# Gated linear attention beside a projection: four gate pieces of a head, one to each half chunk of weights

## The chip, the cores and the metric

The kernel runs on one core of one Trainium2 chip. The metric is the device time of one execution in microseconds (us); the median of three runs of the kernel before is 1993.54 us.

## The reference

One layer of a diffusion backbone: 256 latent tokens and 256 context tokens, width 2048, all in float32. One input projection feeds two token mixers, windowed attention and a bidirectional gated linear attention (GLA) of four heads; their merged output goes through a convolutional FFN. The change touches the GLA alone:

```python
gf = log_sigmoid((lrf @ w_gate_f + b_gate_f)) / GLA_GATE_NORM     # decay, forward; gb the same, backward
...
def step(S, inp):                       # one chunk of 64 tokens, scanned forward and backward
    qc, kc, vc, gc = inp
    b = cumsum(gc)
    o_inter = (qc * exp(b)) @ S
    A[t, s] = sum_d qc[t,d] * kc[s,d] * exp(b[t,d] - b[s,d])      # s <= t
    o = o_inter + A @ vc
    S = exp(b[last]) * S + (kc * exp(b[last] - b)).T @ vc
```

The context gives the states in which the latent scans start. Of each head the key width is 256 and the value width 512.

## The kernel before

Nearly all the time goes into products of the tokens with weights that are read once. Weights come in chunks of 256 rows x 512 columns. ScalarE (ACT) rounds a chunk to `whi` (L227), VectorE (DVE) takes the rest `wlo` (L228), and TensorE (PE) multiplies first with `whi` (the high products), then with `wlo` (the low products). Three buffers each hold `whi` and `wlo`, so the next `whi` can be written only when PE is through with the high products of an earlier chunk, and the next `wlo` only after its low products.

The GLA of a head, without its value product, is a generator, `gla_A`. It runs beside a projection of eight chunks: beside that of the other keys for head 0, beside that of its own values for heads 1 to 3. The projection calls `aside` twice in each chunk, once ahead of the high products (`tick`) and once between high and low ones (`midway`). These 16 places are called slots here: odd ones lie ahead of high products, even ones between high and low. `aside` adds the pace to a sum, and each time that the sum reaches one it lets `gla_A` run on to its next `yield`. PE's instructions of a step are placed behind the last product issued before the slot; those of ACT and DVE are free. A scheduler then settles each engine's order from its own model of times, and every engine works through its order strictly.

The steps of `gla_A` are these. **Gates**: for two directions d and two halves dt of the key width, a product `pz` on PE, then four activations of 128x512 on ACT (L720, L722, L723, L724), then a sum on DVE (L725, into `segs`) and one on GpSimd (POOL, L726, into `gc`). **Levels** 0 to 7: exponentials of `segs` on ACT (L765, L766, and from level 1 on L772, L773), products with queries and keys on DVE (`q2` L767, `k2` L774), and up to four sums on DVE that carry `segs` to the next level (L776 to L779). **Products**: `products(lv)` multiplies `k2` by `q2` of a level on PE into `pa`, and a masked copy on DVE (L750) takes it; called p0 to p7 here. p0 needs only `q2` of level 0. `q2` and `k2` share four buffers, so a level's exponentials wait for the products of the level two below. **End**: two queries, four scans and `kf` (L807), `kg` (L808) on DVE, an empty step, then the final products of `kf` and `kg` on PE (the `pa<-q,kf` of the trace) that give `atc`.

With pace 0.91 the slots of a head hold:

| slot | before |
|---|---|
| 2 | two gates (d = 0) |
| 3 | two gates (d = 1) |
| 4 | first `pa`, level 0 |
| 5 | level 1 |
| 6 | p0 |
| 7 to 11 | levels 2 to 6, each with the product of the level below (p1 to p5) |
| 12 | nothing |
| 13 | level 7, p6 |
| 14 | p7, queries, scans, `kf`, `kg` |
| 16 | final products |

A background job on DVE (L385, 128x1024, some 1.2 us a piece) computes the modulation vectors; the scheduler fits its pieces in between.

Of the kernel before, what the change touches and what calls it, by code (L numbers as in the profile page):

```python
# [30 lines left out]
def layer_kernel(ctx, tc, A, out):  # L31
# [18 lines left out]
    def M(name, shape, dt=F32):  # L50
        return big.tile(shape, dt, name=name, tag="M")

    def W2(tag, name, shape, dt=F32):
        return f2.tile(shape, dt, name=name, tag=tag, bufs=F2_BUFS[tag])

    def bank(name, shape=(P, 512), side=False):

        return ps.tile(list(shape), F32, name=name, tag="side" if side else "main", bufs=3 if side else 1)

    def split(hi, lo, src):  # L60
        S.activation(hi, src, AF.Copy)
        return V.tensor_tensor(lo, src, hi.bitcast(F32), op=ALU.subtract).ins
# [31 lines left out]
    def mm_b(*a, **k):  # L94
        return pe_seq(after(PE.matmul(*a, **k)))  # L95
# [70 lines left out]
    beside = []  # L166
# [537 lines left out]
    def gla_A(h, kb, qb, res):  # L704
        k_ = kb[:, (h % 2) * 2:(h % 2) * 2 + 2, 0:T]
        kc = kb[:, (h % 2) * 2:(h % 2) * 2 + 2, T:2 * T]
        q_ = qb[:, 2 * h:2 * h + 2, :]
        R = M("segs", [P, 4, 2, T])
        PF, SB, SX, PX = (R[:, i] for i in range(4))
        G.memset(R[:, 2:4], 0.0)  # L710
        gc = []
        for d in range(2):
            g_ = W2("fc", "gc", [P, 2, T])
            for dt in range(2):
                f = 2 * h + dt
                pz = bank("pz", side=True)
                mm_b(pz, wg[:, f * P:(f + 1) * P], lr[:, d, :], start=True, stop=True)
                b = nbg[:, d * 8 + f:d * 8 + f + 1]
                e = W2("fb", "ge", [P, 512])
                S.activation(e, pz, AF.Abs, scale=-1.0, bias=b)  # L720
                mn = W2("fb", "gm", [P, 512])
                S.activation(mn, pz, AF.Relu, scale=-1.0, bias=b)  # L722
                S.activation(e, e, AF.Exp, scale=-1.0)  # L723
                S.activation(e, e, AF.Ln, bias=ones[:, 0:1])  # L724
                V.tensor_tensor((PF if d == 0 else SB)[:, dt, :], mn[:, 0:T], e[:, 0:T], op=ALU.add)  # L725
                G.tensor_tensor(g_[:, dt, :], mn[:, T:2 * T], e[:, T:2 * T], op=ALU.add)  # L726
            gc.append(g_)
            yield

        at = sm.tile([P, 2, P], F32, name="at", tag="at", bufs=1)  # L730
        pa = bank("pa", (P, 2, P), side=True)
        for t in range(2):
            for dt in range(2):
                mm_b(pa[:, t, :], k_[:, dt, t * P:(t + 1) * P], q_[:, dt, t * P:(t + 1) * P],
                          start=(dt == 0), stop=(dt == 1))
        V.tensor_scalar(at, pa, 2.0, None, op0=ALU.mult)

        def halves(x, m):
            v = x.rearrange("p d (n two h) -> p (d n) two h", two=2, h=m)
            return v[:, :, 0, :], v[:, :, 1, :]  # L740

        def products(lv, q2, k2):
            pa = bank("pa", (P, 2, P), side=True)
            for t in range(2):
                tq = t if lv < 7 else 1 - t
                for dt in range(2):
                    mm_b(pa[:, t, :], k2[:, dt, t * P:(t + 1) * P],
                              q2[:, dt, tq * P:(tq + 1) * P], start=(dt == 0), stop=(dt == 1))
            if lv < 7:
                V.copy_predicated(at, lmask[:, lv:lv + 1, :].to_broadcast([P, 2, P]), pa)  # L750
            else:
                split(ats[0][:, 0], ats[0][:, 1], at)
                split(ats[1][:, 0], ats[1][:, 1], pa)

        ats = [W2("fc", "ats", [P, 2, 2, P], F32R) for _ in range(2)]
        for lv in range(8):
            m = 1 << lv
            n = T // m
            pfL, pfR = halves(PF, m)
            sbL, sbR = halves(SB, m)  # L760
            sxL, sxR = halves(SX, m)
            pxL, pxR = halves(PX, m)
            q2 = W2("fa", "q2", [P, 2, T])
            qL, qR = halves(q2, m)
            S.activation(qR, pfR, AF.Exp, scale=-1.0 / 16)  # L765
            S.activation(qL, sbL, AF.Exp, scale=-1.0 / 16)  # L766
            V.tensor_tensor(q2, q2, q_, op=ALU.mult)  # L767
            k2 = k_
            if lv:
                k2 = W2("fa", "k2", [P, 2, T])  # L770
                kL, kR = halves(k2, m)
                S.activation(kL, sxL, AF.Exp, scale=-1.0 / 16)  # L772
                S.activation(kR, pxR, AF.Exp, scale=-1.0 / 16)  # L773
                V.tensor_tensor(k2, k2, k_, op=ALU.mult)  # L774
            if lv < 7:
                V.tensor_tensor(sxL, sxL, pfR[:, :, m - 1:m].to_broadcast([P, n, m]), op=ALU.add)  # L776
                V.tensor_tensor(pxR, pxR, sbL[:, :, 0:1].to_broadcast([P, n, m]), op=ALU.add)
            V.tensor_tensor(pfR, pfR, pfL[:, :, m - 1:m].to_broadcast([P, n, m]), op=ALU.add)
            V.tensor_tensor(sbL, sbL, sbR[:, :, 0:1].to_broadcast([P, n, m]), op=ALU.add)  # L779
            if lv == 1:  # L780
                yield
            if lv:
                products(lv - 1, *prev)
            prev = q2, k2
            yield
        products(7, *prev)


        q2 = W2("fa", "q2", [P, 2, T])
        q3 = W2("fa", "q3", [P, 2, T])  # L790
        for dst, e in ((q2, PF), (q3, SB)):
            S.activation(dst, e, AF.Exp, scale=-1.0 / 16)
            V.tensor_tensor(dst, dst, q_, op=ALU.mult)
        kf = W2("fa", "kf", [P, 2, T])
        kg = W2("fa", "kg", [P, 2, T])
        tot = sm.tile([P, 2], F32, name="tot", tag="tot", bufs=2)
        one = ones[:, 0:1].to_broadcast([P, T])
        for dt in range(2):
            V.tensor_tensor_scan(kf[:, dt, :], one, gc[0][:, dt, :], 0.0, op0=ALU.mult, op1=ALU.add)
            V.memset(kg[:, dt, 0:1], 0.0)  # L800
            V.tensor_tensor_scan(kg[:, dt, 1:T], ones[:, 0:1].to_broadcast([P, T - 1]), gc[1][:, dt, 0:T - 1], 0.0,
                                 op0=ALU.mult, op1=ALU.add)
        V.tensor_scalar(tot, kf[:, :, T - 1], -1.0 / 16, None, op0=ALU.mult)
        for dt in range(2):
            S.activation(kf[:, dt, :], kf[:, dt, :], AF.Exp, scale=1.0 / 16, bias=tot[:, dt:dt + 1])
        S.activation(kg, kg, AF.Exp, scale=-1.0 / 16)
        V.tensor_tensor(kf, kf, kc, op=ALU.mult)  # L807
        V.tensor_tensor(kg, kg, kc, op=ALU.mult)  # L808
        yield
        yield  # L810
        pa = bank("pa", (P, 2, T), side=True)
        for t in range(2):
            for i, (kk, qq) in enumerate(((kf, q2), (kg, q3))):
                for dt in range(2):
                    mm_b(pa[:, t, :], kk[:, dt, t * P:(t + 1) * P], qq[:, dt, :],
                              start=(i == 0 and dt == 0), stop=(i == 1 and dt == 1))
        atc = [W2("fc", "atc", [P, 2, T], F32R) for _ in range(2)]
        split(atc[0], atc[1], pa)
        res.extend((ats, atc))
# [32 lines left out]
    qbt = M("qb", [P, 8, T])  # L852
# [2 lines left out]

    def with_gla(h, kb, block):
        res = []
        beside[:] = [gla_A(h, kb, qbt, res), 0.91, 0.0]
        v = block()
        for _ in beside[0]:  # L860
            pass
        beside.clear()
        return res, v

    def kb_block():
        kb = M("kb1", [P, 4, 512])
        proj_T(w_in, KB + 512, ALL, [h_all(0), h_all(1)], lambda i, b: S.activation(kb[:, i, :], b, AF.Copy))
        return kb

    a, kb1 = with_gla(0, kbt, kb_block)  # L870
    v = M("v0h", [P, 4, 512], F32R), M("v0l", [P, 4, 512], F32R)
    for i in range(4):
        split(v[0][:, i, :], v[1][:, i, :], vb0[:, i, :])
    gla_o(0, a, *v)
    for h in (1, 2, 3):
        a, v = with_gla(h, kb1 if h > 1 else kbt, lambda h=h: v_block(VB + h * 512, f"v{h}", h == 3))
        if h < 3:
            gla_o(h, a, *v)
# [424 lines left out]
```

## Time and profile before

| | |
|---|---|
| median of three runs | 1993.54 us (1993.23 to 1993.6) |
| profiled execution | 1993.73 us, of it a span of 1991.7 us |
| PE busy | 1965.2 us (99%) |
| DVE busy | 1401.9 us (70%) |
| ACT busy | 971.1 us (49%) |
| granted TensorE clock | 0.998 |
| GLA heads 0, 1, 2, 3 in the span | from 224, 287, 351, 415 us, each until 52 to 55 us later |

The start of a head is its first `pz` on PE. A wait of PE in this kernel is time lost, since PE is busy almost everywhere. A wait of DVE or ACT costs nothing by itself; it matters where PE later waits for what was held up. In rows of the timeline the number behind `x` counts the instructions merged into the row, and the bracket gives the idle time ahead of it on its engine, with what ended it.

### The profile page before, as it was taken

Reading aid. Unit: us, or ns where it says so; the run is one execution under the profiler, and the core shown is the slowest. Engines: PE = TensorE matmul, PEld = TensorE weight load, DVE = VectorE, ACT = ScalarE, POOL = GpSimd, SP = SyncE. Lnnn points to the kernel's source line nnn. Section 1 sums busy time; section 2 is a strip of 40 time slices with the busy share of each in tenths; the row PEclk is TensorE's granted clock in tenths of the full one; section 3 lists DMA queues with packets and bytes.
Section 4 is the critical chain, followed back from the end, with each engine's and each line's share of the span. In section 5 each row is a group of like instructions: output and inputs, shape, how many; then the busy total and the mean of one; then the engine's idle time right before and its main releaser. Section 6 shows DMA issues by size and latency. Waiting matters only on the chain.

```text
span 1991.7 us, 27308 instructions
## 1 busy us (share of the span) xinstructions
PE 1965.2 (99%) x10393; PEld 1644.6 (83%) x10393; DVE 1401.9 (70%) x2164; ACT 971.1 (49%) x1417; POOL 48.5 (2%) x69
## 2 busy tenths in 40 slices
PE   6999999999999999999999999999999999999999
PEld 5779897878887788888888888888888888888887
DVE  4666568867858898777776458888887555667754
ACT  4323464653345566444444445755555334555532
POOL 1001000111000000000000000000000000000000
PEclk9999999999999999999999999999999999999999
DMA  9987223235754455888888768688886566666563
GB/s 324 385 293 212 66 75 95 85 99 188 241 174 127 117 180 187 269 291 289 291 289 285 237 220 283 180 264 275 270 269 233 195 195 190 188 186 188 189 215 113
DMA packets 199699, 420.89 MB, mean 211 GB/s; under 512 B 12660, under 2 KB 21156, under 8 KB 198416
## 3 DMA queue, kind: packets, MB, share of 16 engines
q1 hardware_dynamic: 197808, 413.25, 64.3%
q0 software_dynamic: 1696, 5.89, 1.0%
q8 instruction: 81, 1.33, 0.3%
q14 instruction: 50, 0.41, 0.1%
q10 hardware_dynamic: 64, 0.02, 0.0%
HBM read 416.97 MB, written 2.13 MB: 210 GB/s over the span
## 4 chain that ended last, share of the span: by engine, by line
PE 93%; DVE 3%; ACT 2%; issue 1%; DMA 1%; POOL 0%; SPq 0%; POOLq 0%; DVEq 0%; ACTq 0%
PE acc L83 71%; PE accs L83 12%; PE pa L95 2%; PE pm L95 1%; PE poa L95 1%; PE pS L95 1%; PE po L95 1%; PE ptp L98 1%; DVE wlo L228 1%; DMA mraw<-in_w_mod 1%; PE plr L677 0%; PE pto L98 0%; ACT ge L720 0%; ACT whi L227 0%; DVE raw L385 0%
## 5 line engine op out<-in xcount | busy, mean ns | idle before, releaser
L228 DVE TENSOR_TENSOR wlo<-raw,whi 128x1024 fp32r<-128x1024 f32 x568 | 694.2, 1223 | 432.2 <-ACT whi L227 392.6
L227 ACT ACTIVATE whi<-raw 128x1024 fp32r<-128x1024 f32 x568 | 601.4, 1059 | 787.7 <-PE acc L83 614.1
L83 PE MATMUL accs<-h,whi 128*128 128x512 f32 x704 | 176.3, 392 | 0.0
L83 PE MATMUL acc<-h,whi 128*128 128x512 f32 x640 | 160.4, 392 | 0.0
L83 PEld LDWEIGHTS accs<-h,whi 128*128 128x128 f32 x704 | 126.6, 189 | 22.6
L83 PE MATMUL acc<-whi,h01hi 128*128 128x512 f32 x352 | 140.0, 398 | 0.0
L83 PE MATMUL acc<-whi,h00hi 128*128 128x512 f32 x352 | 139.1, 395 | 0.0
L83 PE MATMUL acc<-whi,h00lo 128*128 128x512 f32 x352 | 138.0, 392 | 0.0
L83 PE MATMUL acc<-whi,h01lo 128*128 128x512 f32 x352 | 137.8, 392 | 0.0
L83 PE MATMUL acc<-whi,al 128*128 128x512 f32 x352 | 137.0, 389 | 0.0
L83 PE MATMUL acc<-whi,ah 128*128 128x512 f32 x352 | 137.0, 389 | 0.0
L83 PEld LDWEIGHTS acc<-h,whi 128*128 128x128 f32 x640 | 115.1, 189 | 20.6
L83 PEld LDWEIGHTS accs<-h,wlo 128*128 128x128 f32 x704 | 96.0, 190 | 6.9
L83 PE MATMUL acc<-wlo,h01hi 128*128 128x512 f32 x352 | 98.7, 396 | 0.0
L83 PE MATMUL accs<-h,wlo 128*128 128x256 f32 x704 | 98.2, 282 | 0.0
L83 PE MATMUL acc<-wlo,h00hi 128*128 128x512 f32 x352 | 98.0, 395 | 0.0
L83 PE MATMUL acc<-wlo,ah 128*128 128x512 f32 x352 | 94.3, 389 | 0.0
L83 PEld LDWEIGHTS acc<-h,wlo 128*128 128x128 f32 x640 | 87.4, 190 | 6.3
L83 PE MATMUL acc<-h,wlo 128*128 128x256 f32 x640 | 89.4, 282 | 0.0
L385 DVE CUSTOM_DVE_ANT_0 raw<-raw,csrow,c 128x1024 f32<-128x1024 f32 x64 | 81.5, 1281 | 0.0
L83 PEld LDWEIGHTS acc<-whi,h00hi 128*128 128x128 f32 x352 | 66.3, 188 | 14.3 <-issue 0.8
L83 PEld LDWEIGHTS acc<-whi,al 128*128 128x128 f32 x352 | 66.1, 188 | 13.7
(402 smaller groups left out, 3589.6 us busy)
## 6 DMA issues: line engine op xcount, KB each, us to landing
raw<-in_w_in SPq DMA_DIRECT2D x208, 512.0 KB, 4.4
raw<-in_w_up SPq DMA_DIRECT2D x176, 512.0 KB, 3.9
raw<-in_w_modT SPq DMA_DIRECT2D x128, 512.0 KB, 4.6
raw<-in_w_down SPq DMA_DIRECT2D x88, 512.0 KB, 3.9
mraw<-in_w_mod SPq DMA_DIRECT2D x32, 1024.0 KB, 12.9
raw<-in_w_attn_o SPq DMA_DIRECT2D x32, 512.0 KB, 5.0
raw<-in_w_gla_o SPq DMA_DIRECT2D x32, 512.0 KB, 5.1
raw<-in_w_out SPq DMA_DIRECT2D x32, 512.0 KB, 4.9
```

The costliest lines, as they stand in the source:

```text
L83: r = pe_seq(PE.matmul(*a, **k))
L95: return pe_seq(after(PE.matmul(*a, **k)))
L98: return pe_seq(after(PE.transpose(*a)))
L227: j = S.activation(hi[:, 0:n, :], raw[:, 0:n, :], AF.Copy).ins
L228: i = V.tensor_tensor(lo[:, 0:n, :], raw[:, 0:n, :], hi[:, 0:n, :].bitcast(F32), op=ALU.subtract).ins
L385: i0 = V.tensor_tensor_reduce(out=raws[i], in0=raws[i], in1=row[0], scale=1.0, scalar=d if h else bmod[:, b0:b0 + 1], op0=ALU.mult, op1=AL ...
```

## The change

The `yield` behind a direction's gates moves into the loop over halves, so the gates come in four pieces; the second `yield` of level 1, which set level 1 apart from p0, goes; the pace becomes 0.97, which lets a step run in each slot from 2 to 16.

```diff
                 G.tensor_tensor(g_[:, dt, :], mn[:, T:2 * T], e[:, T:2 * T], op=ALU.add)
+                yield
             gc.append(g_)
-            yield
...
             V.tensor_tensor(sbL, sbL, sbR[:, :, 0:1].to_broadcast([P, n, m]), op=ALU.add)
-            if lv == 1:
-                yield
             if lv:
                 products(lv - 1, *prev)
...
-        beside[:] = [gla_A(h, kb, qbt, res), 0.91, 0.0]
+        beside[:] = [gla_A(h, kb, qbt, res), 0.97, 0.0]
```

The slots after the change: 2, 3, 4 and 5 hold one gate each; 6 the first `pa` and level 0; 7 to 13 levels 1 to 7, each with the product of the level below (p0 to p6); 14 and 16 are as before. No instruction is added or taken away, SP's loads and POOL's work keep their order, and outside the GLA's heads no engine's order changes. Lines behind L779 are two less in the kernel after; names below are those of before.

PE in head 1 around p0. `pa_3014` of before and `pa_3022` of after are p0, `pa_2986` is the first `pa`, `pa_3040` is p1; `wlo` rows are the low products of the third chunk. Before:

```order
L83 MATMUL acc_2850<-wlo_2995,h00hi_299 128x512 x2
L83 MATMUL acc_2851<-wlo_2995,h00hi_299 128x512 x2
L95 MATMUL pa_3014<-q2_2959,kb0_117 128x128 x4
L83 MATMUL acc_2852<-wlo_2995,h10hi_301 128x512 x2
L83 MATMUL acc_2853<-wlo_2995,h10hi_301 128x512 x2
L83 MATMUL acc_2850<-whi_3048,h00hi_299 128x512
L83 MATMUL acc_2850<-whi_3048,h00lo_300 128x512
L83 MATMUL acc_2850<-whi_3048,h00hi_299 128x512
L95 MATMUL pa_3040<-q2_2975,k2_2979 128x128 x4
```

And after:

```order
L95 MATMUL pa_2986<-qb_2129,kb0_117 128x128 x4
L83 MATMUL acc_2850<-wlo_2966,h00hi_299 128x512 x2
L83 MATMUL acc_2851<-wlo_2966,h00hi_299 128x512 x2
L83 MATMUL acc_2852<-wlo_2966,h10hi_301 128x512 x2
L83 MATMUL acc_2853<-wlo_2966,h10hi_301 128x512 x2
L95 MATMUL pa_3022<-q2_2994,kb0_117 128x128 x4
```

The first `pa` moves from the second chunk to the third, and p0 from the middle of the third chunk's low products to their end.

ACT in head 1, from the last gate on. `ge_2920` and `ge_2950` are the fourth gate, `q2_2959` and `q2_2994` the queries of level 0, `q2_2975` and `q2_3010` those of level 1. Before:

```order
L723 ACTIVATE ge_2920<-ge_2920 128x512
L765 ACTIVATE q2_2959<-segs_2876 128x256
L724 ACTIVATE ge_2920<-ge_2920,ones_90 128x512
L766 ACTIVATE q2_2959<-segs_2876 128x256
L765 ACTIVATE q2_2975<-segs_2876 128x128x2
L227 ACTIVATE whi_3183<-raw_3181 128x1024
L766 ACTIVATE q2_2975<-segs_2876 128x128x2
```

And after:

```order
L723 ACTIVATE ge_2950<-ge_2950 128x512
L765 ACTIVATE q2_2994<-segs_2876 128x256
L724 ACTIVATE ge_2950<-ge_2950,ones_90 128x512
L765 ACTIVATE q2_3010<-segs_2876 128x128x2
L227 ACTIVATE whi_3165<-raw_3163 128x1024
L766 ACTIVATE q2_2994<-segs_2876 128x256
```

The second exponential of level 0 (L766) moves behind the `whi` of a chunk.

DVE in head 1 over the same stretch; L767 on `q2_2959` or `q2_2994` is the product that p0 needs. Before:

```order
L228 TENSOR_TENSOR wlo_3115<-raw_3112,whi_3114 128x1024
L725 TENSOR_TENSOR segs_2876<-gm_2912,ge_2910 128x256
L385 ISA raw_2989,shift2_109<-raw_2989,csrow_2398,c1_106 128x1024
L385 ISA shift2_109 128x1
L725 TENSOR_TENSOR segs_2876<-gm_2922,ge_2920 128x256
L778 TENSOR_TENSOR segs_2876<-segs_2876 128x256
L777 TENSOR_TENSOR segs_2876<-segs_2876 128x256
L767 TENSOR_TENSOR q2_2959<-q2_2959,qb_2129 128x512
L779 TENSOR_TENSOR segs_2876<-segs_2876 128x256
L767 TENSOR_TENSOR q2_2975<-q2_2975,qb_2129 128x512
```

And after:

```order
L228 TENSOR_TENSOR wlo_3097<-raw_3094,whi_3096 128x1024
L385 ISA raw_2960,shift2_109<-raw_2960,csrow_2380,c1_106 128x1024
L385 ISA shift2_109 128x1
L725 TENSOR_TENSOR segs_2876<-gm_2934,ge_2932 128x256
L778 TENSOR_TENSOR segs_2876<-segs_2876 128x256
L725 TENSOR_TENSOR segs_2876<-gm_2952,ge_2950 128x256
L777 TENSOR_TENSOR segs_2876<-segs_2876 128x256
L736 TENSOR_SCALAR at_2985<-pa_2986 128x256
L767 TENSOR_TENSOR q2_2994<-q2_2994,qb_2129 128x512
L779 TENSOR_TENSOR segs_2876<-segs_2876 128x256
```

The background piece moves ahead of the third gate's sum, and the copy of the first `pa` (L736) moves in ahead of the product; behind it both orders hold the same work in this head. In head 3 four background pieces stand between this product and `kf` before, and three after.

## The prediction

> **What bounds the kernel.** I read the page first, then PE's waits, then the busy time in the stretch of the GLA's heads.
>
> ```profile
> PE 1965.2 (99%) x10393; PEld 1644.6 (83%) x10393; DVE 1401.9 (70%) x2164; ACT 971.1 (49%) x1417; POOL 48.5 (2%) x69
> PE 93%; DVE 3%; ACT 2%; issue 1%; DMA 1%; POOL 0%; SPq 0%; POOLq 0%; DVEq 0%; ACTq 0%
> ```
>
> PE bounds the whole, and the chain that ends last runs on it for 93% of the span. The change adds no product, so it can win only what PE waits in the heads. The list of PE's waits has these two for the GLA (total, times, longest):
>
> ```profile
> PE pa L95 <- DVE kf L807: 2.5, 3, 1.0
> PE pa L95 <- DVE q L767: 2.3, 3, 1.1
> ```
>
> They lie in heads 1 to 3, once each per head, 4.8 us in all: at p0, which waits for the query of level 0, and at the final products, which wait for `kf`. The busy time by stretch agrees for heads 0 and 1 (length, then PE's busy time and instructions):
>
> ```profile
> 215.00:275.00 60.00, 59.90 (x533) 55.75 (x522) 43.26 (x83) 32.70 (x64) 3.91 (x4) 1.00 0.22 64
> 275.00:350.00 75.00, 73.38 (x363) 60.43 (x363) 50.30 (x93) 42.55 (x87) 6.65 (x6) 1.00 0.27 84
> ```
>
> Head 0, in the first row, leaves PE 0.1 us idle, head 1 1.6. Now the two waits in the timeline of PE, head by head (start, length, what):
>
> ```profile
> 286.90 0.62 PE L95 MATMUL pz<-wgl 128*128 128x512 f32 x2
> 301.84 1.16 PE L95 MATMUL pa<-q,kb 128*128 128x128 f32 x8 [1.07 <-DVE q L767]
> 336.88 1.10 PE L95 MATMUL pa<-q,kf 128*128 128x256 f32 x4 [0.54 <-DVE kf L807]
> ...
> 351.35 0.62 PE L95 MATMUL pz<-wgl 128*128 128x512 f32 x2
> 365.57 1.16 PE L95 MATMUL pa<-q,kb 128*128 128x128 f32 x8 [0.36 <-DVE q L767]
> 400.89 1.10 PE L95 MATMUL pa<-q,kf 128*128 128x256 f32 x4 [0.99 <-DVE kf L807]
> ...
> 415.37 0.62 PE L95 MATMUL pz<-wgl 128*128 128x512 f32 x2
> 430.06 1.16 PE L95 MATMUL pa<-q,kb 128*128 128x128 f32 x8 [0.82 <-DVE q L767]
> 466.62 1.10 PE L95 MATMUL pa<-q,kf 128*128 128x256 f32 x4 [0.94 <-DVE kf L807]
> ```
>
> What DVE does between the two waits decides what the first is worth. In head 1:
>
> ```profile
> 291.05 0.43 DVE L725 TENSOR_TENSOR segs<-gm,ge 128x256 f32<-128x256 f32 x1 [0.40 <-ACT ge L724]
> ...
> 297.47 0.97 DVE L725 TENSOR_TENSOR segs<-gm,ge 128x256 f32<-128x256 f32 x1
> 301.11 0.68 DVE L767 TENSOR_TENSOR q<-q,qb 128x512 f32<-128x512 f32 x1
> 302.63 0.69 DVE L767 TENSOR_TENSOR q<-q,qb 128x512 f32<-128x512 f32 x1 [0.51 <-ACT q L766]
> 314.60 0.42 DVE L776 TENSOR_TENSOR segs<-segs 128x256 f32<-128x256 f32 x1 [0.18 <-ACT k L772]
> 317.55 0.45 DVE L750 COPY_PREDICATED at<-lmask,pa 128x256 f32<-128x256 uint8 x1 [0.31 <-PE pa L95]
> 325.56 1.22 DVE L228 TENSOR_TENSOR wlo<-raw,whi 128x1024 fp32r<-128x1024 f32 x1 [0.16 <-issue]
> 336.04 0.69 DVE L807 TENSOR_TENSOR kf<-kf,kb 128x512 f32<-128x512 f32 x1 [0.44 <-ACT kf L805]
> ```
>
> The last five rows have all of DVE's idle times over 0.1 us from the query of level 0 (301.11) to the end of `kf` (336.73): 1.6 us of 35.6. So DVE is the bound between the waits. PE that comes to p0 without waiting comes to the final products earlier and waits there: a head gains what `kf` gains, and no more. The question is when DVE's run begins and whether its idle times go.
>
> **The change part by part.** No instruction comes or goes, so each edit costs only by place. The dropped `yield` adds no wait: p0 needs nothing of level 1, and p0 stands in its slot as before a chunk later. The pace fills the free slot 12 and brings p7 and the final products to the slots they had. What is left is the place of the gates, of level 0 and of p0. I reckon PE's time up to slot 6 from its own rows: two `pz` take 0.62 us and one 0.39, so one takes 0.23; eight low products, sixteen high ones and a `pa` come from the chain of waits:
>
> ```profile
> 317.51 1.84 PE acc L83 x8
> 388.80 0.89 PE pa L95 x8
> 389.69 3.64 PE acc L83 x16
> ```
>
> Slot 6 lies 4 x 0.23 + 2 x 1.84 + 2 x 3.64 = 11.9 us behind the first `pz`, since the first `pa` now follows it. In head 1 that is 298.8. There the new order of ACT puts a `whi` ahead of the exponential that the query needs, and a `whi` waits for PE:
>
> ```profile
> 293.87 1.05 ACT L227 ACTIVATE whi<-raw 128x1024 fp32r<-128x1024 f32 x1
> 297.94 0.72 ACT L724 ACTIVATE ge<-ge,ones 128x512 f32<-128x512 f32 x1
> ...
> 301.23 1.04 ACT L227 ACTIVATE whi<-raw 128x1024 fp32r<-128x1024 f32 x1
> 302.17 0.42 ACT L766 ACTIVATE q<-segs 128x256 f32<-128x256 f32 x1
> ...
> 308.55 1.06 ACT L227 ACTIVATE whi<-raw 128x1024 fp32r<-128x1024 f32 x1 [1.10 <-PE acc L83]
> ```
>
> The `whi` of slot 6 can start at about 298.9; the exponential follows 0.94 later (301.23 to 302.17) and ends after 0.42, at 300.3; the query's product on DVE starts at 300.4 to 300.7 (L736, which now stands ahead of it, needs the first `pa` of slot 6). That is 1.7 us behind slot 6, a figure that I use for every head. The fourth gate is no later. ACT went from the `whi` of slot 4 at 293.87 to the gate's end at 298.66 in 4.8 us, with six gate activations between; now that `whi` can start at slot 4, 286.9 + 2 x 0.23 + 1.84 + 3.64 = 292.8, and eight follow it, the two more at 0.72 at most each: 299.0 at the latest, and its sum on DVE (0.43) before 299.6.
>
> *Head 1.* The query comes at 300.55 in place of 301.11, 0.55 earlier. It ends at 301.2 and PE is at p0 at 298.8 + 0.89 + 1.84 = 301.5: the first wait goes. Of DVE's idle times behind it, 0.51 goes (the exponential of level 1 stood behind that `whi`, and now a `wlo` of DVE lies between), and 0.31 may (p4 had slipped into the next chunk); waits like the 0.18 may come at three more levels, since products now stand a slot later for levels 2 to 6. I take 0.35 as gain, from -0.5 to 0.8. `kf` is 0.9 us earlier, and so is the end of the head.
>
> For the other heads these rows of DVE are needed:
>
> ```profile
> 364.84 0.68 DVE L767 TENSOR_TENSOR q<-q,qb 128x512 f32<-128x512 f32 x1
> 394.33 0.69 DVE L799 TENSOR_TENSOR_SCAN kf<-ones,gc 128x256 f32<-128x256 f32 x1 [0.94 <-PE pa L95]
> 428.42 1.58 DVE L767 TENSOR_TENSOR q<-q,qb 128x512 f32<-128x512 f32 x1
> 436.81 1.27 DVE L385 CUSTOM_DVE_ANT_0 raw<-raw,csrow,c 128x1024 f32<-128x1024 f32 x1
> 464.59 1.28 DVE L385 CUSTOM_DVE_ANT_0 raw<-raw,csrow,c 128x1024 f32<-128x1024 f32 x1
> ```
>
> *Head 2.* Slot 6 is at 351.35 + 11.9 = 363.25, the query at 364.95 in place of 364.84. The first wait of 0.36 goes and `kf` comes no earlier; of the 0.94 before the scans, which wait for p7, at most the same 0.36 goes. I take 0, from -0.4 to +0.4.
>
> *Head 3.* Slot 6 is at 427.25, the query at 428.95 in place of 428.42. But there the row took 1.58 in place of 0.68, beside a sum of POOL:
>
> ```profile
> 428.69 0.75 POOL L726 TENSOR_TENSOR gc<-gm,ge 128x256 f32<-128x256 f32 x1
> ```
>
> If the fourth gate's POOL sum is through by then, the query ends at 429.6 in place of 430.0, 0.4 earlier; if it falls on the query again, 0.5 later. The gate's sum of 0.97 at 297.47 beside that of 0.43 at 291.05 is a like case. The Trainium skill ("SBUF — State Buffer", section "Who interferes with whom") has a rule for it: a VectorE operation with two SBUF inputs and a GpSimd operation that reads SBUF lock one another out, and the later one waits until the first is done. The two long rows agree with it; by the rule head 3 has the late end of the two if POOL starts first. Behind the query the first and last of four background pieces are shown above (436.81 and 464.59); the new order has three there, which takes 1.27 off DVE's run, and one level sum (0.42 in the row of 314.60) that stood ahead of the query stands behind it. That is 0.85 less, so `kf` is 0.35 to 1.25 us earlier, and the two waits of 0.82 and 0.94 have room for it. I take 0.6.
>
> *Head 0.* It had no wait at p0:
>
> ```profile
> 237.42 0.68 DVE L767 TENSOR_TENSOR q<-q,qb 128x512 f32<-128x512 f32 x1
> ...
> 238.25 1.13 PE L95 MATMUL pa<-q,kb 128*128 128x128 f32 x8
> ```
>
> The query ended at 238.10, 0.15 ahead of PE. p0 had slipped behind five high products of the next chunk and now stands ahead of them; the query has one level sum less ahead of it (0.42). If PE gains up to 1 us to p0 and the query up to 0.42, a wait of 0 to 0.5 us appears; I take 0.2.
>
> Sum: 0.2 - 0.9 + 0 - 0.6 = -1.3 us. The profiled execution took 1993.73, 0.19 above the median of 1993.54 (lowest 1993.23); against the median this gives 1992.2, against the profiled execution 1992.4. I take 1992.3. Behind the heads PE's order is the same and it is busy throughout, so a gain arrives whole.
>
> **The rivals.**
>
> *The first waits go and nothing takes their place.* 1.07 + 0.36 + 0.82 = 2.25 us less: 1991.3; with the second waits gone as well 4.7 less, 1988.8. For it: the gates of a slot are halved, and the 0.51 that DVE waited for an exponential goes. The Trainium skill ("Perfetto Trace Analysis", section "Optimizing Scalar/DVE Operations") says for engines that are not saturated yet cause bubbles that breaking work up may end it sooner; by it the time would be this one. Against it: DVE is idle for 1.6 us of 35.6 between the waits, so it is saturated there.
>
> *The query comes late and the head ends later (slower).* Level 0 moves from slot 4 to slot 6, and its exponential waits behind a `whi` that waits for PE. The forecast has 1.7 us from slot 6 to the query. It decides in heads 1 and 2 at 2.3 (301.11) and 1.6 (364.84). If the query needs 2.6, because the first `pa`'s copy or POOL's lock hold it, heads 1 and 2 lose 0.3 and 1.0, head 3, with POOL's sum on its query, 0.6, and head 0 the 0.5: 2.4 us, 1996.0. For it: two of the three margins are under 0.6.
>
> *Nothing changes.* The gains of heads 1 and 3 are eaten by new idle times of DVE at levels 2 to 6: 1993.5, give or take 0.4. For it: DVE's work between the waits is the same to an instruction in heads 1 and 2.
>
> **How the numbers follow.** Forecast 0.45, first waits gone 0.15, late query 0.2, nothing 0.2. The forecast's own terms reach from -3.0 to +0.5, so from 1990.6 to 1994.1 (head 1 from -1.35 to 0, head 2 -0.4 to +0.4, head 3 -1.25 to -0.35, head 0 0 to 0.5). A range of 1990.6 to 1995.2 takes in that, the first rival's lower gain, the case of no change, and the milder half of the late query. About 0.2%, 4 us, is what a measurement of this kernel can tell from no change. Faster by more needs nearly all of the 4.8 us: 0.03. Slower by more needs the late query at nearly twice its price: 0.04. Within: 0.93.
>
> **What would show it.** In the profile after, PE's waits for the query (L767) are gone or under 0.3 us each in heads 1 to 3, those for `kf` stay at 0.6 to 1.3 each, and head 1 from its first `pz` to the final products takes about 49.1 us in place of 49.98, head 2 49.5 as before, head 3 about 50.6 in place of 51.25. ACT's L766 of level 0 follows a `whi` that starts at slot 6. DVE has 4 idle times or more over 0.1 us in the run of head 1. I am wrong if `kf` waits vanish (DVE was not the bound), or if the query starts later than 2.3 us behind slot 6.

## The result and the profile after

The changed kernel takes 1989.1 us (median of 13 runs, 1988.69 to 1989.75), the kernel before 1993.54 (13 runs, 1993.11 to 1994.37): ratio 0.9978, 95% interval 0.9970 to 0.9986. That is 4.4 us faster. The forecast was 1992.3 and its range ended at 1990.6, so more than three times the expected gain came, and the forecast is wrong. The profiled execution has a span of 1987.2 us in place of 1991.7.

First the page's busy row and the list of PE's waits in the GLA (total, times, longest):

```profile
PE 1962.6 (99%) x10393; PEld 1645.1 (83%) x10393; DVE 1401.4 (71%) x2164; ACT 970.5 (49%) x1417; POOL 46.7 (2%) x69
```

```profile
PE pa L95 <- DVE kf L805: 2.7, 3, 1.1
PE pa L95 <- DVE k L774: 0.4, 1, 0.4
```

The waits for the query, 2.3 us in all, are gone. Those for `kf` stayed, and a new one of 0.4 stands at p6 of head 2. The list alone gives 1.7 us of the 4.4. Now the timeline of PE, head by head, the first `pz` and the first final product, with the wait in brackets:

```profile
285.53 0.39 PE L95 MATMUL pz<-wgl 128*128 128x512 f32 x1
297.32 1.05 PE L95 MATMUL pa<-qb,kb 128*128 128x128 f32 x8
300.04 1.08 PE L95 MATMUL pa<-q,kb 128*128 128x128 f32 x8
334.03 1.10 PE L95 MATMUL pa<-q,kf 128*128 128x256 f32 x4 [1.13 <-DVE kf L805]
...
348.52 0.39 PE L95 MATMUL pz<-wgl 128*128 128x512 f32 x1
397.77 1.10 PE L95 MATMUL pa<-q,kf 128*128 128x256 f32 x4 [0.76 <-DVE kf L805]
...
411.82 0.39 PE L95 MATMUL pz<-wgl 128*128 128x512 f32 x1
461.86 1.10 PE L95 MATMUL pa<-q,kf 128*128 128x256 f32 x4 [0.86 <-DVE kf L805]
```

From first `pz` to final products heads 1 to 3 take 48.50, 49.25 and 50.04 us, before 49.98, 49.54 and 51.25: 1.48, 0.29 and 1.21 less. Head 0, from its first `pz` to its last final product in the trace, takes 50.41 in place of 51.34. The four make 3.9 us. Between heads 2 and 3 another 0.4 goes, about half of it because one weight product of 0.23 us that stood behind head 2 now stands inside it. In the stage behind, 0.3 comes back, so the last product in the trace is 4.0 us earlier, counted from the first `pz` of head 0. Of the rest, 0.4 lies ahead of the heads, where the traces of this study differ by up to 0.8 us in no order that could be told.

**Where the rest of the gain was.** Head 0 shows no wait in either kernel. Its gain is seen only in the spacing of single products. Before, at p4 of head 0, PE and then DVE:

```profile
250.94 0.28 PE L83 MATMUL acc<-h11lo,whi 128*128 128x256 f32 x1
251.06 0.28 PE L83 MATMUL acc<-h01hi,wlo 128*128 128x256 f32 x1
251.38 1.13 PE L95 MATMUL pa<-q,k 128*128 128x128 f32 x8
...
250.55 0.69 DVE L774 TENSOR_TENSOR k<-k,kb 128x512 f32<-128x512 f32 x1
```

A product of this head starts 0.12 us behind the one ahead of it (250.94 to 251.06), but p4 starts 0.32 behind: PE stopped for 0.20. Its record hides it, since each product is recorded for 0.28 us and overlaps the next by 0.16, so PE reads as busy and no wait is listed beyond what shows as idle. The operand `k` ended at 251.24, 0.14 ahead of p4. The same place after:

```profile
251.74 0.28 PE L83 MATMUL acc<-h01hi,wlo 128*128 128x256 f32 x1
251.86 0.28 PE L83 MATMUL acc<-h11hi,wlo 128*128 128x256 f32 x1
251.98 1.05 PE L95 MATMUL pa<-q,k 128*128 128x128 f32 x8
...
249.72 0.68 DVE L774 TENSOR_TENSOR k<-k,kb 128x512 f32<-128x512 f32 x1
```

p4 stands in a later slot, its operand ended 1.58 us ahead, the spacing is 0.12, and the eight products take 1.05 in place of 1.13. I worked this out for p0 to p7 of all heads in both traces, from the starts of all products less the usual spacing, and from the end of the later operand. A product that waits for its operand starts 0.06 to 0.15 us behind the operand's end in these rows, so a stop of this kind shows as a small distance between the two. Before, 16 of 32 products have it under 0.2 us ahead, and these 16 hold all of the 4.87 us that PE stops there, 1.1 of it between their own eight parts; the other 16 hold nothing. After, 6 of 32 are so close, and the stops are 1.1 us. A stop is from here on what PE is late by this spacing, listed as a wait or not.

### The profile page after: what moved, and what is told of

It reads as the page before. It is cut to its first block, busy times and chain, and to the rows that moved or that the text cites. A ratio compares the mean times of both kernels' runs of the same rounds, so it can differ in the third digit from the quotient of the medians.

```text
span 1987.2 us, 27312 instructions
## 1 busy us (share of the span) xinstructions
PE 1962.6 (99%) x10393; PEld 1645.1 (83%) x10393; DVE 1401.4 (71%) x2164; ACT 970.5 (49%) x1417; POOL 46.7 (2%) x69
## 4 chain that ended last, share of the span: by engine, by line
PE 92%; DVE 5%; ACT 2%; issue 1%; DMA 1%; POOL 0%; SPq 0%; ACTq 0%; DVEq 0%; POOLq 0%
PE acc L83 71%; PE accs L83 12%; PE pa L95 2%; PE pm L95 1%; PE poa L95 1%; PE pS L95 1%; DVE wlo L228 1%; PE po L95 1%; PE ptp L98 1%; DMA mraw<-in_w_mod 0%; DVE k L774 0%; DVE q L767 0%; ACT whi L227 0%; PE plr L677 0%; PE pto L98 0%
## 5 line engine op out<-in xcount | busy, mean ns | idle before, releaser
L228 DVE TENSOR_TENSOR wlo<-raw,whi 128x1024 fp32r<-128x1024 f32 x568 | 695.4, 1225 | 431.8 <-ACT whi L227 394.6
L385 DVE CUSTOM_DVE_ANT_0 raw<-raw,csrow,c 128x1024 f32<-128x1024 f32 x64 | 81.7, 1285 | 0.0
```

The lines of the kernel that those rows point to most:

```text
L228: i = V.tensor_tensor(lo[:, 0:n, :], raw[:, 0:n, :], hi[:, 0:n, :].bitcast(F32), op=ALU.subtract).ins
L385: i0 = V.tensor_tensor_reduce(out=raws[i], in0=raws[i], in1=row[0], scale=1.0, scalar=d if h else bmod[:, b0:b0 + 1], op0=ALU.mult, op1=AL ...
```

## The experiments

Most of them replace the pace by a list: how many steps of `gla_A` run in slots 1 to 16.

```diff
-        if beside:
+        if len(beside) == 2:
+            for _ in range(beside[1].pop(0) if beside[1] else 0):
+                next(beside[0], None)
+        elif beside:
...
-        beside[:] = [gla_A(h, kb, qbt, res), 0.97, 0.0]
+        beside[:] = [gla_A(h, kb, qbt, res), [<list>]]
```

Level 1 has its own step again in the lists, so the changed kernel reads 0 1 1 1 1 1 2 1 1 1 1 1 1 1 1 1. Lines behind L228 are three to five more in these kernels. "Just in time" counts the products p0 to p7 whose operand ends under 0.2 us ahead, of 32; their stops and those at the final products are sums over four heads, from the traces.

| kernel | us, median | ratio to before, 95% | just in time | stops p0 to p7 | stops at `kf` |
|---|---|---|---|---|---|
| before | 1993.5 | | 16 | 4.87 | 2.96 |
| changed | 1989.1 | 0.9970 to 0.9986 | 6 | 1.11 | 3.23 |
| pairs_late | 1990.8 | 0.9979 to 0.9996 | 4 | 2.63 | 3.14 |
| pairs_early_levels_late_products | 1991.08 | 0.9980 to 0.9998 | 5 | 1.79 | 4.15 |
| spread_early | 1991.15 | 0.9980 to 0.9998 | 16 | 3.95 | 2.51 |
| p0_early | 1991.79 | 0.9983 to 1.0001 | 4 | 3.15 | 3.47 |
| pairs_apart | 1989.25 | 0.9970 to 0.9988 | 6 | 1.26 | 3.29 |
| before_nobg | 1992.57 | 0.9987 to 1.0005 | 14 | 4.46 | 2.47 |
| after_nobg | 1988.7 | 0.9970 to 0.9987 | 4 | 0.15 | 3.39 |
| nobg_piece_behind_kf | 1987.65 | 0.9960 to 0.9982 | 4 | 0.16 | 2.40 |
| after_ones | 1988.9 | 0.9967 to 0.9986 | 2 | 0.40 | 3.46 |
| slot_earlier | 1990.72 | 0.9978 to 0.9995 | 13 | 4.66 | 1.37 |
| slot_earlier_nobg | 1987.4 | 0.9956 to 0.9980 | 8 | 2.50 | 0.01 |
| end_earlier_nobg | 1989.36 | 0.9972 to 0.9990 | 8 | 4.13 | 0.54 |

In each of these traces the products just in time hold all of the stops, to 0.03 us. The intervals are 0.16 to 0.24% wide, wider than the scatter of a kernel's own runs (most within 0.5 us of their median).

**The parts of the change, each alone.** `pairs_late` puts the gates back in pairs:

```diff
-0 1 1 1 1 1 2 1 1 1 1 1 1 1 1 1
+0 2 2 0 0 1 2 1 1 1 1 1 1 1 1 1
```

> The four gates go in two pairs in slots 2 and 3, as in the kernel before; the first pa with level 0 at slot 6 and all products stand as in the changed kernel. Slack theory (the products stand a slot further behind their operands, and TensorE's short stops at them and the wait at p0 go): nearly the whole gain stays, 1989 to 1990. Gate theory (the four single gates bring it, since a pair holds VectorE and ScalarE back): most of the gain is lost, 1992 to 1993.5, and heads 1 to 3 show waits at the first gated products again. Theory of the prediction (a head gains what kf gains): like the changed kernel where kf comes as early; a pair done earlier would bring kf no later, so 1989 to 1990 too.

`pairs_early_levels_late_products` is the kernel before with p0 to p5 a slot later; levels 2 to 6, which share their steps, move with them:

```diff
-0 2 2 1 1 1 1 1 1 1 1 0 1 1 1 1   (the kernel before)
+0 2 2 1 1 0 1 1 1 1 1 1 1 1 1 1
```

> Gates in pairs, level 0 at slot 4 and level 1 at slot 5 as in the kernel before; p0 at slot 7 and p1 to p5 a slot later than before, up to slot 12, which was empty. The products are moved alone. Slack theory: the short stops (0.05 to 0.3 us each) and the waits at p0 go, 1989 to 1990. Gate theory: nothing of the gates is changed, so 1993 to 1994. Theory of the prediction: VectorE's run is that of the kernel before, so kf is where it was and only the wait moves from p0 to kf: 1993 to 1994.

`spread_early` has the gates one by one, the products where they were:

```diff
-0 2 2 1 1 1 1 1 1 1 1 0 1 1 1 1   (the kernel before)
+0 1 1 1 2 2 1 1 1 1 1 0 1 1 1 1
```

> The gates go one by one in slots 2 to 5 as in the changed kernel, then two steps a slot in slots 5 and 6, so that p0 to p5 stand in the slots of the kernel before and slot 12 is empty. Slack theory: p0 and the products after it have their operands just in time or late (level 0 is now only a slot ahead of p0), so the stops stay or grow: 1993 to 1996. Gate theory: the gain stays, 1989 to 1990. Theory of the prediction: between them, 1992 to 1994, by what kf gains.

Measured 1990.80, 1991.08 and 1991.15: each part brings about half, 2.2 to 2.5 of 4.4 us, and neither theory holds alone. The lists of PE's waits tell what each half is, first of `spread_early`, then of the kernel with late products:

```profile
PE pa L95 <- DVE q L770: 1.3, 3, 0.5
```

```profile
PE pa L95 <- DVE kf L810: 3.7, 3, 1.5
```

With single gates the query's product ends 0.2, 0.6 and 0.2 us earlier in heads 0, 1 and 3 (0.15 later in head 2), counted from the first `pz`, and the waits at p0 fall from 2.3 to 1.3 while 16 products stay just in time. Late products take away the stops at p0 to p7 (4.87 to 1.79), and `kf` takes 1.2 us of it back.

`p0_early` moves p1 to p5, with the levels in their steps, and leaves p0:

```diff
-0 2 2 1 1 1 1 1 1 1 1 0 1 1 1 1   (the kernel before)
+0 2 2 1 1 1 0 1 1 1 1 1 1 1 1 1
```

> The kernel before with its products p1 to p5 a slot later (slot 12 filled, slot 7 empty); gates in pairs, levels 0 and 1 and p0 in the slots of before. Slack theory: the waits at p0 stay as in the kernel before (0.5 to 1.2 us in heads 1 to 3, 2.7 in sum), the short stops at p1 to p5 go (1.2 to 1.6 us): 1991.5 to 1992.3. If it was p0's slot that brought the 2.2 us of the run with all products later, this one gives nothing: 1993 to 1993.6.

Measured 1991.79, 1.7 less than before, though its interval just takes in no change. Its list of PE's waits has p0 as it was:

```profile
PE pa L95 <- DVE q L770: 2.2, 3, 1.1
```

The stops at p1 to p7, 1.68 us before and listed nowhere, are 0 in its trace. So the slack theory holds for them to 0.1 us, and they are a gain of their own.

**Why single gates help.** `pairs_apart` leaves a slot between two pairs:

```diff
-0 2 2 0 0 1 2 1 1 1 1 1 1 1 1 1   (pairs_late)
+0 2 0 2 0 1 2 1 1 1 1 1 1 1 1 1
```

> As the changed kernel, but the gates in two pairs in slots 2 and 4 (pairs in slots 2 and 3 gave 1990.8). If it is the burst of two pairs in neighbouring slots that delays ScalarE's weights and the query (p0 waits 2.3 us in sum there, 0 in the changed kernel), a slot between them helps: 1989 to 1989.8. If a pair costs by itself, because two gates' sums on VectorE lie beside GpSimd's of the same gates and take twice their time, or TensorE stops between a pair's two products: 1990.3 to 1991.2.

Measured 1989.25: all of the gain of single gates, with pairs. The timeline of ACT in head 1 shows it, the `whi` of slot 4 and the query's exponential, first of `pairs_late` (first `pz` at 286.64), then of `pairs_apart` (285.72):

```profile
286.64 0.61 PE L95 MATMUL pz<-wgl 128*128 128x512 f32 x2
...
293.62 1.06 ACT L230 ACTIVATE whi<-raw 128x1024 fp32r<-128x1024 f32 x1
298.84 0.45 ACT L768 ACTIVATE q<-segs 128x256 f32<-128x256 f32 x1 [0.43 <-DVE segs L781]
300.47 0.42 ACT L769 ACTIVATE q<-segs 128x256 f32<-128x256 f32 x1
```

```profile
285.72 0.61 PE L95 MATMUL pz<-wgl 128*128 128x512 f32 x2
...
291.81 1.06 ACT L230 ACTIVATE whi<-raw 128x1024 fp32r<-128x1024 f32 x1
299.10 0.43 ACT L769 ACTIVATE q<-segs 128x256 f32<-128x256 f32 x1
```

With two pairs in neighbouring slots the weights' copy starts 6.98 us behind the first `pz` in place of 6.09, since ACT has two activations of the second pair ahead of it, and the query's exponential 13.83 in place of 13.38. A pair as such costs nothing that can be told (1989.25 beside 1989.1); two pairs in neighbouring slots cost 1.6 us. By the traces that loss does not lie in head 1, whose rows show the delay: from first `pz` to final products it takes 48.70 us in `pairs_late` and 48.67 in `pairs_apart`. It lies in head 0 (48.38 in place of 47.16), where the query comes 2.1 us later and p0 stops for 0.9, and in head 3 (51.66 in place of 50.02), where the query comes 0.5 later and DVE has four background pieces of 1.3 us up to `kf` in place of three; part of it comes back in head 2 and behind the heads. So the late query is seen to cost time in head 0, while in head 3 the place of a piece has a share that no run tested alone. The Trainium skill ("Perfetto Trace Analysis", section "Optimizing Scalar/DVE Operations") says of engines that are not saturated that breaking up instructions may let work end sooner. Here no instruction was broken up, and a gap between whole pairs was enough.

**What bounds the heads now.** `before_nobg` and `after_nobg` take the background pieces out of the heads. `bg_rate` holds the pieces per tick and their running sum; the rate goes from 0.3 to 0.0 there and from 0.52 to 0.62 later:

```diff
-    bg_rate[:] = [0.3, 0.0]
+    bg_rate[:] = [0.0, 0.0]
...
-    bg_rate[0] = 0.52
+    bg_rate[0] = 0.62
```

> The kernel before, without the background pieces beside the heads (they go to the stages behind, whose later rate rises from 0.52 to 0.62); slots, gates and products as in the kernel before. VectorE is then up to 1.2 us ahead for each piece that stood between the query and kf. Slack theory (TensorE's stops are waits for operands that come just in time): where pieces are gone, from p2 or p3 on in heads 1 to 3, the stops of 0.1 to 0.2 us at the products shrink and kf waits go, while head 0, which has no piece in its run, keeps its 1.7 us of short stops and the waits at p0 stay at 0.5 to 1.2 us: 1990.5 to 1992.5. If a product inside a chunk of weights costs its stop by its position alone, not by its operands, the short stops stay in all heads and only kf's waits change: 1992 to 1993.5.

> The changed kernel without the background pieces that run beside the heads (0.3 a slot; they go to the stage behind the heads, whose rate rises from 0.52 to 0.62). VectorE and ScalarE have less between the query of level 0 and kf. Theory of the prediction (VectorE's run sets kf, kf sets the head's end): the waits of 0.9 to 1.3 us at the final products of heads 1 to 3 shrink or go, 2 to 2.7 us less, 1986.5 to 1987.5, if the stage behind can take the pieces. Slack theory: the same for the waits at kf, nothing more for the short stops. If the stage behind the heads is the fuller one, the pieces come back there: 1989 to 1991.

The kernel before gains 0.9 us by the medians (1992.57, not told from no change, and a little above the range of the slack theory): 14 products stay just in time, because the schedule still sets them right behind their operands. This run does not settle position against operands. Seven products in the traces of before and of `spread_early` do: they stand inside a chunk with 0.26 to 0.35 us of slack, and their stops are 0.00. The changed kernel without pieces takes 1988.7, as good as the same, where the theory of the prediction had 1986.5 to 1987.5. In its trace the products behind head 2 are 1.6 us earlier than in that of the changed kernel, and those behind head 3 are 0.8 later. The timeline of PE and DVE there, then the busy time by stretch (length, PE, PEld, DVE, ACT, POOL, granted clock, DMA):

```profile
461.08 1.61 PE L95 MATMUL pa<-q,kf 128*128 128x256 f32 x4 [1.93 <-DVE kf L805]
...
457.52 0.16 DVE L801 TENSOR_SCALAR tot<-kf 128x2 f32<-128x2 f32 x1
458.80 1.28 DVE L385 CUSTOM_DVE_ANT_0 raw<-raw,csrow,c 128x1024 f32<-128x1024 f32 x1
460.00 0.94 DVE L805 TENSOR_TENSOR kf<-kf,kb 128x512 f32<-128x512 f32 x1
```

```profile
459.00:461.00 2.00, 0.15 (x1) 0.00 (x0) 2.00 (x4) 0.59 (x2) 1.84 (x2) 1.00 0.72 244
461.00:462.00 1.00, 0.92 (x3) 0.82 (x4) 1.00 (x2) 0.00 (x0) 1.00 (x4) 0.77 0.91 225
462.00:463.00 1.00, 1.00 (x4) 0.75 (x3) 0.13 (x1) 0.00 (x0) 1.00 (x4) 0.50 0.76 299
463.00:464.00 1.00, 1.00 (x4) 0.81 (x3) 0.00 (x0) 0.00 (x0) 1.00 (x5) 0.50 0.00 0
464.00:466.00 2.00, 2.00 (x8) 1.66 (x8) 0.00 (x0) 0.00 (x0) 0.29 (x2) 0.76 0.00 0
466.00:468.00 2.00, 2.00 (x11) 1.64 (x10) 0.69 (x1) 1.50 (x3) 0.00 (x0) 1.00 0.00 0
```

A piece of the stage behind (L385) stands ahead of `kf`, PE is idle for 1.93, and then its clock is halved for some 3.4 us: by the shares 0.77 and 0.76 in the rows at both ends, from 461.5 to 465.0. `nobg_piece_behind_kf` starts those pieces two ticks later, by a running sum that begins at minus two times the rate:

```diff
-    bg_rate[0] = 1.6
+    bg_rate[:] = [1.6, -3.2]
```

> The changed kernel without background pieces beside the heads, and with the stage behind them starting its pieces two ticks later, so that the first piece of 1.3 us stands behind kf of head 3 on VectorE and not ahead of it. Theory: that piece was all that held kf of head 3 in the run without background pieces (kf at 49.4 us behind the head's first pz against 47.4 in heads 1 and 2), so the wait of 2.1 us falls to 0.6 to 0.9, and the 2.1 us that TensorE lost behind it at half its pace (final products 0.43 us apart in place of 0.22) go with it if the long stop caused them: 1985.2 to 1986.8. If the half pace has another cause: 1986.8 to 1987.6. If the stage behind loses what the heads gain: 1988 to 1989.

Measured 1987.65, 1.0 less, where 2 to 3.5 was expected. By the traces it is more: the stop at head 3 is 1.1 us (forecast 0.6 to 0.9) with no half pace behind it, and the last product is 2.4 us earlier than without the edit, as the two profiled runs are 2.7 us apart (1990.29 and 1987.60). The runs without the edit spread over 2.2 us, from 1988.14 to 1990.35, those with it over 0.4. So the half pace probably fell into the profiled run and a few of the others only; their clock in the heads was not recorded, and that is argued, not shown.

**Moving the side work earlier.** `after_ones` has one step in each slot; `slot_earlier` all but the final products a slot earlier than in the changed kernel:

```diff
-0 1 1 1 1 1 2 1 1 1 1 1 1 1 1 1   (the changed kernel)
+1 1 1 1 1 1 1 1 1 1 1 1 1 1 1 1   (after_ones)
+1 1 1 1 1 2 1 1 1 1 1 1 1 1 0 1   (slot_earlier)
```

> The changed kernel with one step in every slot: the four gates in slots 1 to 4, level 0 at slot 5, level 1 at slot 6, p0 at slot 7, all else as changed. Slack theory: p0, whose operand in the changed kernel ended 0.06 to 0.14 us ahead of it, gets 2 us of slack, and kf, if VectorE's run starts a slot earlier, waits less: kf waits of 0.9 to 1.3 fall by up to 1 us a head: 1986.5 to 1989. If the run is bound by ScalarE and by its own length from the first whi on, nothing is gained: 1989 to 1989.6. If the first gate collides with the products of the head before: 1990 to 1992.

> All of a head's side work of the changed kernel a slot earlier: single gates in slots 1 to 4, level 0 at slot 5, level 1 with p0 at slot 6, p1 to p7 a slot earlier; only the final products stay in slot 16. If kf is late because VectorE's run from the query on is full and starts when level 0's slot comes, kf is 2 us earlier and the waits at the final products (3.2 us in three heads) go, with p0 just in time as in the changed kernel: 1986 to 1987. If VectorE or ScalarE are so full in front of the query that it comes no earlier, kf stays and p0 waits about 1 to 2 us a head: 1990 to 1993.

`after_ones` gives 1988.9, the same as the changed kernel: the stops at p0 to p7 fall by 0.7 us, and `kf` takes a third of it back (3.46). `slot_earlier` gives 1990.72: the stops at `kf` fall to 1.37, and those at p0 to p7 grow to 4.66, with 13 products just in time again. `slot_earlier_nobg` is the same list with both background edits, `end_earlier_nobg` the changed kernel's with both edits and p7's step in slot 13:

```diff
-0 1 1 1 1 1 2 1 1 1 1 1 1 1 1 1   (the changed kernel)
+1 1 1 1 1 2 1 1 1 1 1 1 1 1 0 1   (slot_earlier_nobg)
+0 1 1 1 1 1 2 1 1 1 1 1 2 1 0 1   (end_earlier_nobg)
```

> The same without background pieces beside the heads, and with the stage behind starting its pieces two ticks later. In the runs without pieces the waits at kf were 0.65 us in heads 1 and 2, the same with the slots of the kernel before and of the changed one, so something other than VectorE's run sets them there. If that is the slot of p7 and of the sums that lead to kf, they go with the slot: 2.4 us less than the 1987.65 of the run with late pieces, 1985 to 1986. If not, 1987.3 to 1988.

> The changed kernel without pieces beside the heads and with late pieces behind them (1987.65), and with p7 and the sums that lead to kf in slot 13, with level 7, in place of slot 14. Gates, level 0 and p0 to p6 stay. If the slot of those sums sets kf once VectorE has nothing else to do, the stops at the final products of heads 1 to 3 (0.65, 0.65 and 1.10 us) go, and p7, slid into a chunk just in time, costs 0.1 to 0.3 us a head: 1985.5 to 1986.8. If VectorE's run sets kf even so, the stops stay: 1987.4 to 1988.3.

`slot_earlier_nobg` gives 1987.4, with 1987.65 the best of the study and not told apart from it: no stop at `kf` at all, but 2.5 us at p0 to p7. `end_earlier_nobg` gives 1989.36, worse than the 1987.65 that it started from. PE's waits there:

```profile
PE pa L95 <- DVE k L777: 3.0, 4, 0.9
PE pa L95 <- DVE kf L810: 0.4, 1, 0.4
```

The stop left `kf` and went to p7, whose operand was now just in time, and `kf` itself came no earlier (47.14 us behind the first `pz` of head 1, against 47.00). In that head DVE is idle for only 1.7 of the 33.5 us from the query to `kf`. So it is not the slot of the last sums that sets `kf`, but DVE's run, even without pieces.

## Why the prediction was wrong

**What held.** The waits for the query are gone, those for `kf` are 0.76 to 1.13. Slot 6 lies 11.79 us behind the first `pz` (forecast 11.9), and ACT's L766 follows a `whi` there, at 297.81. The rule "a head gains what `kf` gains" holds to 0.01 us in heads 1 to 3 of the traces. DVE in head 1, the query, the idle times of its run and `kf`:

```profile
299.21 0.69 DVE L767 TENSOR_TENSOR q<-q,qb 128x512 f32<-128x512 f32 x1
307.55 0.42 DVE L776 TENSOR_TENSOR segs<-segs 128x256 f32<-128x256 f32 x1 [0.17 <-ACT k L772]
311.85 0.43 DVE L776 TENSOR_TENSOR segs<-segs 128x256 f32<-128x256 f32 x1 [0.17 <-ACT k L772]
315.02 0.43 DVE L776 TENSOR_TENSOR segs<-segs 128x256 f32<-128x256 f32 x1 [0.17 <-ACT k L772]
333.19 0.69 DVE L805 TENSOR_TENSOR kf<-kf,kb 128x512 f32<-128x512 f32 x1 [0.38 <-ACT kf L803]
```

The query starts 13.68 us behind the first `pz` in place of 14.21, 0.53 earlier (forecast 0.55). `kf` starts 47.66 behind it in place of 49.14, 1.48 earlier, and the head is 1.48 shorter. The four idle times that were to be seen are there.

**What failed first: "PE can win only what it waits in the heads", with 4.8 us from the list of waits.** The list and the busy rows leave out stops that a product's record covers. By spacing, PE stopped 7.8 us at p0 to p7 and at the final products, not 4.8, and 1.7 of the 3.0 that were missing lie at p1 to p7. Head 0 shows it: there the forecast was 0.2 us of loss, argued from a query just ahead of p0. The query did come just in time again (it ended 0.13 ahead, no stop over 0.03), and the stops at p0 to p5, which the prediction did not see, fell from 0.68 to 0.03, with 0.3 more at the gates' `pz`. The query kept pace with PE: it starts 0.94 us earlier behind the first `pz`, where 0.42 at most was allowed. With +0.2 in place of -0.93 this step alone is 1.1 us. The whole gain stays under the 4.8, but only 1.7 of it came out of the list.

**What was mis-sized: the length of DVE's run.** Head 1: the run from query to `kf` got 0.95 shorter where 0.35 was taken (34.93 to 33.98 us); its idle times over 0.1 fell from 1.60 to 0.89, and the rest is smaller idle times and slightly shorter rows. The bound of the range, 0.8, was close. Head 2: the wait of 0.94 in front of the scans, of which 0.36 was allowed, is gone; `kf` is 0.3 earlier, where 0 was taken, though the query comes 0.19 later and one level sum more stands behind it (the prediction has DVE's work there as the same to an instruction). Head 3: 1.21 where 0.6 was taken, at the upper end of its 0.35 to 1.25: `kf` has three pieces ahead as forecast, and POOL's sum did not fall on the query again, which took 0.67 in place of 1.58. It fell on a level sum ahead of the query, which took 1.01 in place of some 0.4:

```profile
424.35 1.01 DVE L777 TENSOR_TENSOR segs<-segs 128x256 f32<-128x256 f32 x1
425.62 0.67 DVE L767 TENSOR_TENSOR q<-q,qb 128x512 f32<-128x512 f32 x1
```

POOL's sum runs there from 424.31 to 425.06. So the query ended only 0.16 us earlier, behind the first `pz`, where 0.4 was the better of the two cases. Of the row of 1.58 in the kernel before, the prediction says that it agrees with the rule it quotes; but that row starts at 428.42, ahead of POOL's at 428.69, so it does not show which of the two came first.

Together heads 1 to 3 gave 3.0 in place of 1.5. The prediction's own terms allowed them that much at most. Beyond its lowest sum, -3.0, lie the 0.93 of head 0 and some 0.5 outside the heads; the 0.5 stays open.

The two errors may have a root in common: a product just in time makes PE stop, and the step of DVE that reads that product (L750 before, with 0.31 us of idle in front of it) comes late as well. Late products alone bring `kf` of head 1 only 0.4 us, so this is at most a part, and it is argued, not shown. The prediction saw moved slots only as new waits for DVE ("waits like the 0.18 may come at three more levels").

**The rivals.** "The second waits go as well", at 1988.8, lies near the result, but by the wrong way: the waits at `kf` stayed. "The query comes late": it comes 1.89 us behind slot 6 in head 1, under the 2.3 at which it decides there. In head 2, where it decides at 1.6, the query was late, by 0.19, and `kf` still came earlier. "Nothing changes" fell with its argument, since DVE's work to an instruction the same took 0.95 us less.

**What stays open.** The two halves of the change add up in time, but not head by head: `kf` comes earlier by this much, in us:

| | head 1 | head 2 | head 3 |
|---|---|---|---|
| single gates (`spread_early`) | 1.0 | 0.1 | 0.2 |
| late products | 0.4 | 0.9 | 0.0 |
| both (the change) | 1.5 | 0.3 | 1.2 |

In head 3 a piece that falls out of the run may tell it: DVE has four between the query and `kf` in the kernel before and in each half alone, three in the changed kernel and in `pairs_apart`. No run tested that alone.

## What to carry to other kernels

Read a saturated engine's stops from the spacing of its starts, not from its list of waits: where records overlap, stops of 0.1 to 0.2 us vanish, and here the unlisted part was 3.0 us beside 4.8 listed. In a schedule written by slots, give each consumer a slot of slack behind its operand (here 0.26 us and more was without a stop), and keep steps of the same kind out of neighbouring slots where another engine's feed (here the weights' copy) has to pass. When waits are removed one by one, follow the run that sets the end of the stage: at `kf` it took back 1.2 of the 3.1 us that late products alone had freed, and in `end_earlier_nobg` the stop only changed its place.

## What the runs showed of the hardware

An idle time of PE of 1.93 us in `after_nobg` was followed by a granted clock of 0.50 in the rows from 462 to 464 us, where the final products start 0.43 us apart in place of 0.22. From the first to the last of the sixteen final products 5.00 us pass, and 3.31 in `nobg_piece_behind_kf`: that is 1.7 us on top of the idle time, not the 2.1 that was reckoned with there. A shorter one, of 1.46 us, left the clock whole in the kernel with late products:

```profile
464.40 1.10 PE L95 MATMUL pa<-q,kf 128*128 128x256 f32 x4 [1.46 <-DVE kf L810]
...
466.00:468.00 2.00, 2.00 (x11) 1.77 (x10) 2.00 (x4) 0.00 (x0) 2.00 (x3) 1.00 0.35 136
```

The Trainium skill ("TensorE: Matmul & The Clock Gate", section "Part 1: The HAM clock gate") gives half speed after at least one idle window of about 3.4 us, in windows that run free; this trace differs in the length, since PE was idle for 1.93 us only and busy up to 459.1, and half speed lasted some 3.4 us. By how much idle time in a window the clock falls, no run here shows.

A product of eight parts whose operand ends under 0.2 us ahead also loses a little inside: in the traces before and after it takes 1.08 to 1.16 us (1.13 at p4 of head 0 before), and 1.05 or 1.06 with more slack.
